# Splitting two weight loads of the last expert but one, and moving a register read behind expert 8's loads

## The chip, the cores and the metric

The kernel runs on one core of one Trainium2 chip. The metric is the device time of one execution in microseconds (us). TensorE (PE) multiplies, VectorE (DVE), ScalarE (ACT) and GpSimd (POOL) do the elementwise work, SyncE (SP) issues nearly all loads from device memory. Before the change three executions took 1123.03, 1123.43 and 1123.51 us; the median is 1123.43 us. A difference of 0.2% (about 2.2 us) is what such a measurement can tell from no change.

## The reference

One layer over 256 tokens of width 1024: a modulated RMS norm, one input projection shared by a convolution branch and a bidirectional linear recurrence, an output projection with a gated residual; then a second modulated norm and a mixture of 32 experts, of which every token takes two out of one group of eight; at the end a gated residual and a final RMS norm. All is float32. The part that the change touches is the mixture:

```python
def swiglu_expert(xb, w1, w3, w2):
    return (jax.nn.silu(xb @ w1) * (xb @ w3)) @ w2

def hier_moe(h, wg, bg, we, be, w1, w3, w2):
    ...                         # group, two experts and gates of each token
    yb = lax.map(run, (xb, blk_e)).reshape(n_rows, D)      # run: swiglu_expert of each block
    return jnp.zeros_like(h).at[tok_buf].add(yb * gate_buf[:, None])
```

Each expert has three matrices of 1024 x 1024 float32, 4 MB each; all 96 are read once, 403 MB.

## The kernel before

**Front part.** The first 198 us hold norms, projections, convolution, recurrence and routing. Every expert then gets 64 token slots (`CAP`). Should an expert have more tokens than that, a loop at the program's end (`rest`) does the remainder; whether it runs is decided by `nmax`, the largest token count, which `nc.values_load` reads into a register of every engine (line 1038). With these inputs the loop doesn't run.

**Experts.** The loop over e = 0 to 30 does for each expert `up(w1)`, SiLU, `up(w3)`, a product, four transposes, and `up(w2)`. `up` reads its matrix in two tiles of 128 partitions x 4096 float32, that is 16 KB in each partition and 2048 KB in all (line 874), and issues eight matmuls for each tile (line 877). So there are 6 such loads for an expert and 186 in the loop. For odd e the gather of the next four experts' tokens stands between `up(w3)` and `up(w2)` (line 789), for even e the scatter of the two experts before (lines 899, 904).

**The ring of tiles.** The tiles are nine buffers, `wide0` to `wide8`, taken in a fixed order (`WORDER`). A load may start once PE has done with the tile that used the buffer nine loads earlier. SP issues all loads in program order, and it stops at the first instruction whose wait isn't over. The loads' completion semaphores are eight, used in rotation (`DMAHW0` to `DMAHW7` below): a load also waits until the load eight before it has landed.

**The token count.** After expert 1, DVE reduces the slot positions to one number (lines 1031 to 1036), with one transpose on PE in between, and writes it to `fmi`. Behind the loads of expert 2, every engine's own queue holds the register read of `fmi` (line 1038); behind it SP issues a small load of the final gain `fgbc` (line 1040), which two matmuls of expert 2's end use (line 1043).

**The last expert.** Expert 31 is loaded in smaller pieces: eight of 1024 KB (line 1059, matmuls in line 1062), four of 512 KB with 4 KB in a partition (line 1106), and four of 512 KB by columns (line 1115; matmuls of both in line 1100). After the last pieces come the scatter (line 1131), the norm and the store of the output.

Of the kernel before, what the change touches and what calls it, by code (L numbers as in the profile page):

```python
# [17 lines left out]
E = 32  # L18
# [51 lines left out]
def hybrid_layer(ctx: ExitStack, tc: tile.TileContext, sp_d, x_d, c_d, bada_d, rb_d, fg_d, gw_d,  # L70
# [3 lines left out]
    dma = nc.sync.dma_start  # L74
# [10 lines left out]
    def bank():  # L85
        return psp.tile([128, 512], F32, name="bank")

    def slot():
        return wp.tile([128, 2048], F32, name="slot")
# [82 lines left out]
    xs = [slot().rearrange("p (k t) -> p k t", k=8) for _ in range(2)]  # L172
# [76 lines left out]
    def load_wz(q):  # L249
        w, hi, lo = slot(), slot_r(), slot_r()  # L250
        dma(w.rearrange("p (k n) -> p k n", k=2),
            win_d[q * 256:(q + 1) * 256, 0:1024].rearrange("(k p) n -> p k n", p=128))
        wz.append([v.rearrange("p (k n) -> p k n", k=2) for v in (hi, lo)])
        return w, hi, lo
# [25 lines left out]
    def slot_r():  # L280
        return r(slot())
# [59 lines left out]
    w = load_wz(0)  # L341
# [3 lines left out]
    for q in range(4):  # L345
        ks = range(2 * q, 2 * q + 2)
        if q < 3:
            w = load_wz(q + 1)
# [9 lines left out]
    for i in range(2):  # L358
        w, hi, lo = slot(), slot_r(), slot_r()
# [173 lines left out]
    def rowbc(dst, rows, j0):  # L533
        for j in range(2):
            pr = bank()
            r = 32 * (j0 + j)
            P.matmul(pr, ones[r:r + 1, :], rows[r:r + 1, :], start=True, stop=True, tile_position=(r, 0))
            S.copy(dst[:, j * 512:(j + 1) * 512], pr)
# [230 lines left out]
    def onehot(oh, t, g):  # L769
        V.tensor_tensor(oh[:, t], iota1[:, None, :].to_broadcast([128, 4, CAP]),  # L770
                        posm[:, t, g * 4:g * 4 + 4, None].to_broadcast([128, 4, CAP]), OP.is_equal)
# [12 lines left out]
    def quad(k):  # L784

        return slice(k // 4 * 512 + k % 4, k // 4 * 512 + 512, 4)

    def gather_mm(pg, i, k, oh, t):
        P.matmul(pg[:, i * 256:(i + 1) * 256], xn[:, t, quad(k)],  # L789
                 oh[:, t].rearrange("p e s -> p (e s)"), start=t + i == 0, stop=t == 1 and i == 1,  # L790
                 skip_group_check=True)

    def gather_out(xg, pg, i, k):
        if i == 0:
            S.activation(xg[:, k], pg[:, i * 256:(i + 1) * 256], AF.Identity, scale=gsp[:, 0, k:k + 1],  # L795
                         bias=gsp[:, 1, k:k + 1])
        else:
            V.tensor_scalar(xg[:, k], pg[:, i * 256:(i + 1) * 256], gsp[:, 0, k:k + 1], gsp[:, 1, k:k + 1],  # L798
                            OP.mult, OP.add)

    def gather_new(dt=F32):
        return (ohp.tile([128, 2, 4, CAP], dt, name="oh"),
                xgt().rearrange("p (k s) -> p k s", k=8))
# [18 lines left out]
    def route(t):  # L822
# [5 lines left out]
                 w=load_wl, z=gelu_mm, e=gelu_act, m=lru_out, M=ln_mean,  # L828
# [5 lines left out]
    for word in ORDER.split():  # L834
        word, _, n = word.partition("*")
# [13 lines left out]
    def wide():  # L849
        n = WORDER[turn[0] % WIDE]  # L850
        turn[0] += 1
        return wx.tile([128, 4096], F32, name=f"wide{n}")
# [14 lines left out]

        return piece

    def up(w_d, e, xs):  # L870
        ps = bank()
        for k4 in range(2):
            w = wide().rearrange("p (k n) -> p k n", k=4)
            dma(w, w_d[e, k4 * 512:(k4 + 1) * 512, :].rearrange("(p k) n -> p k n", p=128))
            for i in range(4):
                for h in range(2):
                    P.matmul(ps[64 * h:64 * h + 64, :], xs(k4 * 4 + i), w[:, i, h * 512:(h + 1) * 512],  # L877
                             start=k4 + i == 0, stop=k4 * 4 + i == 7, tile_position=(0, 64 * h))
        return ps

    def sel_build(e0):
        so = mo.tile([128, 2, 2, CAP], F32, name="so")
        for t in range(2):
            for i in range(2):
                V.tensor_scalar(so[:, t, i], iota1, posm[:, t, e0 + i:e0 + i + 1],
                                gate[:, t, e0 + i:e0 + i + 1], OP.is_equal, OP.mult)
        return so

    def sel_turn(so):
        pt = bank()  # L890
        for t in range(2):
            P.transpose(pt[:, t * 128:(t + 1) * 128], so[:, t].rearrange("p e s -> p (e s)"), ident)
        st = mo.tile([128, 256], F32, name="st")
        S.copy(st, pt[:, 0:256])
        return st

    def scatter_mm(st, yy, t, h):
        pz = bank()
        P.matmul(pz, st[:, t * 128:(t + 1) * 128], yy[:, h * 512:(h + 1) * 512], start=True, stop=True)  # L899
        return pz  # L900

    def scatter_add(pz, t, h):
        q = slice(h * 512, (h + 1) * 512)
        V.tensor_tensor(x1[:, t, q], x1[:, t, q], pz, OP.add)  # L904
# [64 lines left out]
    for e in range(E - 1):  # L969
        xs = lambda k: xg[:, k, (e % 4) * CAP:(e % 4 + 1) * CAP]  # L970
        if e % 2 == 0:
            so = sel_build(e)
        gat = e % 2 == 1 and e // 4 < E // 4 - 1
        if gat and e % 4 == 1:
            noh, nxg = gather_new()
            onehot(noh, 0, e // 4 + 1)
            onehot(noh, 1, e // 4 + 1)
        pa = up(w1_d, e, xs)
        sl = mo.tile([128, 512], F32, name="sl", bufs=1)
        S.activation(sl, pa, AF.Silu)  # L980
        if e == 0:
            rowbc(g2bc, g2r, 2)
        if e % 2 == 0:
            st = sel_turn(so)
        pb = up(w3_d, e, xs)
        gg = sl
        V.tensor_tensor(gg, sl, pb, OP.mult)  # L987
        pzs = []
        k0 = (e % 4) // 2 * 4
        if gat:  # L990
            pgs = [bank(), bank()]
            for k in range(3):
                for t in range(2):
                    gather_mm(pgs[k // 2], k % 2, k0 + k, noh, t)
            for k in range(2):
                gather_out(nxg, pgs[0], k, k0 + k)
        elif e % 2 == 0 and e:
            for n in range(3):
                pzs.append(scatter_mm(*prev, *TH[n]))
                if n < 2:  # L1000
                    scatter_add(pzs[n], *TH[n])
        pt = bank()
        for j in range(4):
            P.transpose(pt[:, j * 128:(j + 1) * 128], gg[:, quad(j)], ident)  # L1004
        gt = mo.tile([128, 4, 128], F32, name="gt", bufs=1)
        V.tensor_copy(gt[:, 0:2], pt[:, 0:256])  # L1006
        S.copy(gt[:, 2:4], pt[:, 256:512])  # L1007
        if gat:
            for t in range(2):
                gather_mm(pgs[1], 1, k0 + 3, noh, t)  # L1010
            for k in range(2, 4):
                gather_out(nxg, pgs[1], k % 2, k0 + k)
        elif pzs:
            pzs.append(scatter_mm(*prev, *TH[3]))
            for n in range(2, 4):
                scatter_add(pzs[n], *TH[n])
        gts = lambda f: gt[:, f % 4, 64 * (f // 4):64 * (f // 4) + 64]
        py = up(w2_d, e, gts)
        if e % 2 == 0:
            yy = mo.tile([128, D], F32, name="yy", bufs=1)  # L1020
        for h in range(2):
            o = (e % 2) * 64
            V.tensor_tensor(yy[o:o + 64, h * 512:(h + 1) * 512], py[64 * h:64 * h + 64, :],  # L1023
                            g2bc[64 * h:64 * h + 64, h * 512:(h + 1) * 512], OP.mult)
        if e % 2 == 1:
            prev = (st, yy)
        if e % 4 == 3:
            xg = nxg
        if e == 1:
            fmx = mo.tile([128, 1], F32, name="fmx")  # L1030
            V.tensor_reduce(fmx, posm.rearrange("p t e -> p (t e)"), AX.X, OP.max)
            fpt = bank()
            P.transpose(fpt[0:1, 0:128], fmx, ident)
            fmr = mo.tile([1, 1], F32, name="fmr")
            V.tensor_reduce(fmr, fpt[0:1, 0:128], AX.X, OP.max)
            V.tensor_copy(fmi, fmr)
        if e == 2:
            nmax = nc.values_load(fmi[0:1, 0:1], min_val=0, max_val=T)
        if e == 2:
            dma(fgbc[0:1, :], fg_d)  # L1040
            for j in range(2):
                pr = bank()
                P.matmul(pr, ones[0:1, :], fgbc[0:1, j * 512:(j + 1) * 512], start=True, stop=True)
                S.copy(fgbc[:, j * 512:(j + 1) * 512], pr)
# [8 lines left out]
    e = E - 1  # L1053
# [49 lines left out]
    for f2 in range(2):  # L1103
        w = piece(2048).rearrange("p (k n) -> p k n", k=2)
# [120 lines left out]
```

## Time and profile before

| what | value |
|---|---|
| time, median of 3 runs | 1123.43 us |
| the profiled execution's own time | 1124.29 us |
| its span, first to last instruction | 1122.5 us |
| PE busy | 1001.9 us, 89% |
| DVE, ACT, POOL busy | 308.7, 173.7, 104.1 us |
| moved by DMA | 445.21 MB, 397 GB/s over the span |
| mean granted PE clock | 0.984 of full speed |

The span is cut into stretches by the views below. "DMA share" is the mean busy share of the core's 16 DMA engines in a stretch; it can come out a little over 1 because a packet is counted where it starts. The chain of waits is followed back from the last instruction, at each step to what released it. A wait that the profile puts down to an instruction ended when that instruction's semaphore was updated.

### The profile page before, as it was taken

The numbers are of one execution on the slowest core, as the hardware profiler recorded it, in microseconds if no ns is written. First come the engines' busy times: TensorE is split into PE (matmuls) and PEld (weight loads), VectorE is DVE, ScalarE is ACT, GpSimd is POOL, SyncE is SP. The second block draws the span as 40 slices with busy tenths as digits, with TensorE's granted clock in tenths as the row PEclk, the third lists the DMA queues.
The fourth block names the chain that finished last, engine by engine and source line by source line (L and its number), as shares of the span: only waits on it lengthen the run. The fifth ranks groups of instructions, "written<-read, shape, count | busy, mean of one in ns | idle before, by whom it ended". The sixth has DMA issues, their size and how long they took to land.

```text
span 1122.5 us, 11836 instructions
## 1 busy us (share of the span) xinstructions
PE 1001.9 (89%) x4947; PEld 447.2 (40%) x4947; DVE 308.7 (27%) x625; ACT 173.7 (15%) x329; POOL 104.1 (9%) x107
## 2 busy tenths in 40 slices
PE   7889999999999999888888998988898989898795
PEld 6764547343434333323333333333333333232244
DVE  4788975221121112111211121112121111111113
ACT  3457944100000000000000000000000000000002
POOL 2487443000000000000000000000000000000001
PEclk9899997999999999999999999999999999999999
DMA  9756759989999999999999999999999999999994
GB/s 362 266 227 267 295 214 409 391 371 411 431 430 431 430 431 430 430 431 431 429 431 430 431 432 430 430 431 430 430 431 430 430 431 430 431 431 430 431 410 184
DMA packets 50015, 445.21 MB, mean 397 GB/s; under 512 B 4083, under 2 KB 14371, under 8 KB 24100
## 3 DMA queue, kind: packets, MB, share of 16 engines
q1 hardware_dynamic: 49746, 443.84, 94.2%
q8 instruction: 41, 0.67, 0.2%
q10 hardware_dynamic: 210, 0.55, 0.1%
q14 instruction: 18, 0.15, 0.0%
HBM read 443.32 MB, written 1.05 MB: 396 GB/s over the span
## 4 chain that ended last, share of the span: by engine, by line
DMA 57%; PE 33%; DVE 5%; POOL 1%; issue 1%; ACT 1%; SPq 1%; DVEq 0%; POOLq 0%; ACTq 0%
DMA wide<-in_w_dram 57%; PE bank L877 18%; PE bank L789 3%; PE bank L680 2%; PE bank L899 2%; PE bank L377 2%; PE bank L331 1%; PE bank L511 1%; DVE bank L469 1%; PE bank L815 1%; PE bank L315 1%; DVE slot L293 1%; PE bank L1004 1%; POOL slot L303 1%; SPq L1059 1%
## 5 line engine op out<-in xcount | busy, mean ns | idle before, releaser
L877 PE MATMUL bank<-wide,xg 128*64 128x512 f32 x1984 | 448.4, 596 | 78.6 <-DMA wide<-in_w_dram 78.5
L877 PEld LDWEIGHTS bank<-wide,xg 128*64 128x64 f32 x1984 | 141.4, 137 | 370.1 <-issue 256.7
L877 PE MATMUL bank<-wide,gt 128*64 128x512 f32 x992 | 219.9, 595 | 2.9 <-DMA wide<-in_w_dram 2.3
L987 DVE TENSOR_TENSOR sl<-sl,bank 128x512 f32<-128x512 f32 x31 | 21.3, 687 | 467.4 <-issue 443.8
L877 PEld LDWEIGHTS bank<-wide,gt 128*64 128x64 f32 x992 | 68.6, 137 | 141.8 <-issue 137.4
L1023 DVE TENSOR_TENSOR yy<-bank,g2bc 64x512 f32<-64x512 f32 x62 | 42.7, 688 | 193.4 <-PE bank L877 193.0
L1142 POOL TENSOR_TENSOR xg<-x,fgbc 128x256 f32<-128x256 f32 x6 | 4.2, 728 | 914.1 <-DMA wide<-in_w_dram 912.8
L980 ACT ACTIVATE sl<-bank 128x512 f32<-128x512 f32 x31 | 18.5, 597 | 437.5 <-PE bank L877 437.5
L789 PE MATMUL bank<-oh,xn 128*128 128x256 f32 x224 | 61.1, 416 | 0.0
L789 PEld LDWEIGHTS bank<-oh,xn 128*128 128x128 f32 x224 | 54.4, 327 | 11.4 <-issue 11.4
L899 PE MATMUL bank<-yy,st 128*128 128x512 f32 x120 | 58.0, 606 | 0.0
L1007 ACT COPY gt<-bank 128x256 f32<-128x256 f32 x31 | 11.6, 373 | 219.4 <-DVE gt L1006 219.4
L904 DVE TENSOR_TENSOR x<-x,bank 128x512 f32<-128x512 f32 x60 | 39.7, 683 | 7.1 <-PE bank L899 7.1
L795 ACT ACTIVATE xg<-bank,gsp 128x256 f32<-128x256 f32 x32 | 17.9, 564 | 153.7 <-PE bank L789 149.2
L303 POOL TENSOR_TENSOR slot<-slot 128x2048 fp32r<-128x2048 f32 x7 | 32.3, 4627 | 34.1 <-ACT slot L298 24.9
L331 PE MATMUL bank<-slot 128*128 128x256 f32 x192 | 28.7, 309 | 7.6 <-ACT slot L292 6.4
L899 PEld LDWEIGHTS bank<-yy,st 128*128 128x128 f32 x120 | 20.6, 191 | 26.5 <-issue 23.2
L331 PEld LDWEIGHTS bank<-slot 128*128 128x128 f32 x192 | 26.5, 211 | 9.7 <-ACT slot L292 7.4
L798 DVE TENSOR_SCALAR xg<-bank,gsp 128x256 f32<-128x256 f32 x32 | 17.2, 543 | 47.3 <-ACT xg L795 47.2
L377 PE MATMUL bank<-slot 128*128 128x512 f32 x96 | 22.9, 394 | 1.5 <-POOL slot L303 1.5
L1004 PEld LDWEIGHTS bank<-ident,sl 128*128 128x128 f32 x124 | 19.5, 204 | 11.1 <-issue 7.1
L487 POOL TENSOR_TENSOR xn<-xn,fgbc 128x256 f32<-128x256 f32 x30 | 22.5, 750 | 2.3
(249 smaller groups left out, 690.1 us busy)
## 6 DMA issues: line engine op xcount, KB each, us to landing
wide<-in_w_dram SPq DMA_DIRECT2D x186, 2048.0 KB, 38.7
slot<-in_wada_dram SPq DMA_DIRECT2D x16, 1024.0 KB, 6.2
slot<-in_wada_dram SPq DMA_DIRECT2D x16, 512.0 KB, 8.8
slot<-in_win_dram SPq DMA_DIRECT2D x8, 1024.0 KB, 9.1
wide<-in_w_dram SPq DMA_DIRECT2D x8, 1024.0 KB, 22.6
slot<-in_wout_dram SPq DMA_DIRECT2D x4, 1024.0 KB, 8.7
wide<-in_w_dram SPq DMA_DIRECT2D x8, 512.0 KB, 11.8
x<-in_x_dram SPq DMA_DIRECT2D x2, 512.0 KB, 4.4
```

The source lines that it names most:

```text
L303: en.tensor_tensor(lo, w, f(hi), OP.subtract)
L331: P.matmul(pvg[ct][:, i * T:(i + 1) * T], wz[k // 2][wi][:, k % 2, c:c + 128], x[k // 4][:, k % 4, 0:T], start=k + i + n == 0, stop=k == 7 ...
L377: P.matmul(pu, w, x[k // 4][:, k % 4], start=k + n == 0, stop=k == 7 and n == 2)
L487: G.tensor_tensor(acc, acc, p, OP.add)
L680: P.matmul(p, m[:, q], w[:, c:c + 512], start=first and n == 0, stop=len(done) == 8 and n == len(passes) - 1)
L789: P.matmul(pg[:, i * 256:(i + 1) * 256], xn[:, t, quad(k)], oh[:, t].rearrange("p e s -> p (e s)"), start=t + i == 0, stop=t == 1 and i == ...
L877: P.matmul(ps[64 * h:64 * h + 64, :], xs(k4 * 4 + i), w[:, i, h * 512:(h + 1) * 512], start=k4 + i == 0, stop=k4 * 4 + i == 7, tile_positi ...
L899: P.matmul(pz, st[:, t * 128:(t + 1) * 128], yy[:, h * 512:(h + 1) * 512], start=True, stop=True)
L904: V.tensor_tensor(x1[:, t, q], x1[:, t, q], pz, OP.add)
L987: V.tensor_tensor(gg, sl, pb, OP.mult)
L1004: P.transpose(pt[:, j * 128:(j + 1) * 128], gg[:, quad(j)], ident)
L1023: V.tensor_tensor(yy[o:o + 64, h * 512:(h + 1) * 512], py[64 * h:64 * h + 64, :], g2bc[64 * h:64 * h + 64, h * 512:(h + 1) * 512], OP.mult)
```

## The change

Two edits. `up` gets the numbers of partitions that its two tiles' main loads cover. For expert 30's `w2` they are 96 and 112 in place of 128 and 128; the remaining 32 and 16 partitions come by loads of 8 partitions each, four and two. The bytes are the same. And the register read of the token count is issued for e = 8 in place of e = 2.

```diff
-    def up(w_d, e, xs):
+    def up(w_d, e, xs, parts=(128, 128)):
+
         ps = bank()
         for k4 in range(2):
             w = wide().rearrange("p (k n) -> p k n", k=4)
-            dma(w, w_d[e, k4 * 512:(k4 + 1) * 512, :].rearrange("(p k) n -> p k n", p=128))
+            src = w_d[e, k4 * 512:(k4 + 1) * 512, :].rearrange("(p k) n -> p k n", p=128)
+            dma(w[0:parts[k4]], src[0:parts[k4]])
+            for o in range(parts[k4], 128, 8):
+                dma(w[o:o + 8], src[o:o + 8])
...
-        py = up(w2_d, e, gts)
+        py = up(w2_d, e, gts, (96, 112) if e == E - 2 else (128, 128))
...
-        if e == 2:
+        if e == 8:
             nmax = nc.values_load(fmi[0:1, 0:1], min_val=0, max_val=T)
```

SP's queue behind expert 2's last loads, before (`wide3`, `wide8`: expert 2's `w2`; `fmi`: the token count; `wide0`, `wide7`: expert 3's `w1`):

```order
L874 DMA wide3_2011<-in_w2_dram 128x4096
L874 DMA wide8_2021<-in_w2_dram 128x4096
L1038 TENSOR_LOAD fmi_1740
L1038 ISA x2
L1040 DMA fgbc_111<-in_fg_dram 1x1024
L874 DMA wide0_2056<-in_w1_dram 128x4096
L874 DMA wide7_2066<-in_w1_dram 128x4096
```

The same place on SP in the changed kernel:

```order
L876 DMA wide3_2011<-in_w2_dram 128x4096
L876 DMA wide8_2021<-in_w2_dram 128x4096
L1044 DMA fgbc_111<-in_fg_dram 1x1024
L876 DMA wide0_2042<-in_w1_dram 128x4096
L876 DMA wide7_2052<-in_w1_dram 128x4096
```

The register read is gone from here; the load of `fgbc` and expert 3's loads follow expert 2's directly. SP's queue behind expert 8's last loads in the changed kernel (`wide3`, `wide8`: expert 8's `w2`; `wide0`, `wide7`: expert 9's `w1`):

```order
L876 DMA wide3_2589<-in_w2_dram 128x4096
L876 DMA wide8_2599<-in_w2_dram 128x4096
L1042 TENSOR_LOAD fmi_1740
L1042 ISA x2
L876 DMA wide0_2631<-in_w1_dram 128x4096
L876 DMA wide7_2641<-in_w1_dram 128x4096
```

The read now stands here, and in the other engines' queues at the same place of the program. SP's queue at expert 30's `w2` and the first loads of expert 31, with the semaphores that each load waits for, before (the first two rows are expert 30's `w2`):

```order
L874 DMA wide_4688<-in_w_dram 128x4096 [waits DMAHW5_49,PE_49]
L874 DMA wide_4698<-in_w_dram 128x4096 [waits DMAHW6_49,PE_49]
L1059 DMA wide_4717<-in_w_dram 128x4x512 [waits DMAHW7_49,PE_49]
L1059 DMA wide_4717<-in_w_dram 128x4x512 [waits DMAHW0_49]
L1059 DMA wide_4738<-in_w_dram 128x4x512 [waits DMAHW1_49,PE_49]
```

And in the changed kernel (the first eight rows are expert 30's `w2`):

```order
L876 DMA wide_4688<-in_w_dram 96x4096 [waits DMAHW5_49,PE_49]
L878 DMA wide_4688<-in_w_dram 8x4096 [waits DMAHW6_49]
L878 DMA wide_4688<-in_w_dram 8x4096 [waits DMAHW7_49]
L878 DMA wide_4688<-in_w_dram 8x4096 [waits DMAHW0_49]
L878 DMA wide_4688<-in_w_dram 8x4096 [waits DMAHW1_49]
L876 DMA wide_4702<-in_w_dram 112x4096 [waits DMAHW2_49,PE_49]
L878 DMA wide_4702<-in_w_dram 8x4096 [waits DMAHW3_49]
L878 DMA wide_4702<-in_w_dram 8x4096 [waits DMAHW4_49]
L1063 DMA wide_4723<-in_w_dram 128x4x512 [waits DMAHW5_49,PE_49]
L1063 DMA wide_4723<-in_w_dram 128x4x512 [waits DMAHW6_49]
```

Two loads have become eight, and all eight semaphores have gone round once: expert 31's first load waits for the semaphore of the 96-partition load, where before it waited for that of a load of expert 29.

## Rows read from the trace of the kernel before

**Rows 1.** The page, part 2: DMA share in tenths and GB/s, 40 equal slices.
```profile
DMA  9756759989999999999999999999999999999994
GB/s 362 266 227 267 295 214 409 391 371 411 431 430 431 430 431 430 430 431 431 429 431 430 431 432 430 430 431 430 430 431 430 430 431 430 431 431 430 431 410 184
```
**Rows 2.** The page, part 4: the chain of waits, shares of the span by engine.
```profile
DMA 57%; PE 33%; DVE 5%; POOL 1%; issue 1%; ACT 1%; SPq 1%; DVEq 0%; POOLq 0%; ACTq 0%
```
**Rows 3.** The chain in order of time: start us, us, what.
```profile
372.36 3.61 PE bank L877 x16
375.99 35.48 DMA wide<-in_w_dram
...
1067.54 3.68 PE bank L877 x16
...
1092.59 12.83 DMA wide<-in_w_dram
...
1105.46 1.09 PE bank L1100 x16
```
**Rows 4.** SP's timeline, 226 to 256 us: start us, us, line, operation, tile, count.
```profile
226.39 7.20 SPq L874 DMA_DIRECT2D wide<-in_w_dram  x3
251.77 0.31 SPq L1040 DMA_DIRECT2D fgbc<-in_fg_dram  x1
252.18 2.14 SPq L874 DMA_DIRECT2D wide<-in_w_dram  x4
```
**Rows 5.** SP's waits, 225 to 256 us: us in total, times, longest us.
```profile
SPq L1038 <- DVE so L885: 17.7, 1, 17.7
```
**Rows 6.** Windows: length, busy of PE PEld DVE ACT POOL, PEclk, DMA share, GB/s.
```profile
246.00:248.00 2.00, 2.00 (x12) 0.53 (x8) 0.00 (x0) 0.00 (x0) 0.00 (x0) 1.00 1.01 434
248.00:250.00 2.00, 0.27 (x2) 0.00 (x0) 1.60 (x3) 0.00 (x0) 0.00 (x0) 1.00 0.33 139
250.00:252.00 2.00, 1.91 (x9) 0.71 (x11) 1.31 (x6) 0.00 (x0) 0.00 (x0) 1.00 0.02 8
252.00:254.00 2.00, 2.00 (x12) 0.72 (x10) 0.00 (x0) 0.00 (x0) 0.00 (x0) 1.00 0.49 109
254.00:256.00 2.00, 2.00 (x12) 0.65 (x10) 0.00 (x0) 0.00 (x0) 0.00 (x0) 1.00 0.97 385
```
**Rows 7.** PE's timeline, 231 to 256 us.
```profile
236.58 3.18 PE L789 MATMUL bank<-oh,xn 128*128 128x256 f32 x12
...
241.18 7.09 PE L877 MATMUL bank<-wide,gt 128*64 128x512 f32 x32
```
**Rows 8.** Line 1038: duration ns min/median/max, first and last start us.
```profile
L1038 SPq TENSOR_LOAD <-fmi x1: 466/466/466, 250.9 to 250.9; - x1
...
L1038 PEldq TENSOR_LOAD <-fmi x1: 490/490/490, 271.4 to 271.4; - x1
L1038 DVEq TENSOR_LOAD <-fmi x1: 545/545/545, 275.9 to 275.9; - x1
```
**Rows 9.** DMA issues: queue, operation, count, KB each, median us to landing.
```profile
wide<-in_w_dram SPq DMA_DIRECT2D x186, 2048.0 KB, 38.7
...
bada<-in_bada_dram ACTq DMA_DIRECT2D x1, 24.0 KB, 3.4
```
**Rows 10.** Windows of the steady state and of the last loads, columns as in rows 6.
```profile
600.00:610.00 10.00, 10.00 (x42) 3.69 (x38) 3.68 (x6) 0.37 (x1) 0.00 (x0) 1.00 1.01 431
...
1104.00:1106.00 2.00, 1.63 (x26) 1.42 (x28) 0.58 (x2) 0.00 (x0) 0.00 (x0) 1.00 0.59 208
1106.00:1108.00 2.00, 2.00 (x24) 1.45 (x20) 1.35 (x4) 0.32 (x1) 0.22 (x1) 1.00 0.23 73
```
**Rows 11.** The page, part 3: packets, MB, share of 16 engines' span.
```profile
q8 instruction: 41, 0.67, 0.2%
```
**Rows 12.** SP's waits over the whole span.
```profile
SPq L874 <- DMA wide<-in_w_dram: 566.1, 141, 5.8
```
**Rows 13.** Line 874 on SP: duration ns min/median/max, first and last start.
```profile
L874 SPq DMA_DIRECT2D wide<-in_w_dram x186: 327/328/425, 155.4 to 1036.9; - x186
```

## The prediction

> **What bounds the kernel now.** I read the page's slices first, then the chain of waits, then SP's timeline and waits where the slices dip, and last the windows around the dip and around the end. From slice 11 to slice 38 the slices show one flat rate, 429 to 432 GB/s with all 16 DMA engines busy [rows 1]; 57% of the chain is the weight loads [rows 2], and from 376 us on the chain is load after load [rows 3], to the last pieces at 1105 us. Before 376 us PE sets the chain, because nine tiles were loaded ahead while PE was still on the front part, and it works off that stock. So after about 200 us the end of the program hangs on one thing: when the stream of loads has moved its last byte. An idle stretch of that stream is paid for in full, wherever it lies, since PE catches up with the stream at 372 us and then only waits for it. After the last pieces there is a tail of PE, ACT and DVE work from 1105.46 us to the end at 1122.5 us, which neither edit touches.
>
> The stream has one hole in that part. SP issues three loads up to 233.6 us and the next at 251.8 us [rows 4]; between them it waits 17.7 us for the token count [rows 5]. What had been issued runs out: the share is 1.01 up to 248 us, then 0.33, 0.02 and 0.49 in steps of 2 us, and 0.97 again from 254 us [rows 6].
>
> **Moving the register read.** It removes SP's 17.7 us stop. What is late next is the buffer: the load behind the read reuses the tile that PE gives back when expert 1's `w3` is done, at about 236.6 us, where the gather begins [rows 7]; the next two reuse the tiles of expert 1's `w2`, given back at 244.7 and 248.3 us (half and all of 241.18 + 7.09). A 2048 KB load takes 2.097 MB / 431 GB/s = 4.87 us. The stream has work until about 248.7 us as it is (a third of the window from 248 to 250); the load at 236.6 carries it to 253.5, the one at 244.7 to 258.4, the one at 248.3 to 263.3. Each is issued about 9 us or more before the stream needs it, so the hole closes.
>
> Its size, by engine time: (1.01 - 0.33) + (1.01 - 0.02) + (1.01 - 0.49) + (1.01 - 0.97) = 2.23, times 2 us = 4.5 us. By bytes: (431 - 139) + (431 - 8) + (431 - 109) + (431 - 385) = 1083, times 2 / 431 = 5.0 us. The engine that finished last gains less than the mean, because in the kernel before all engines start again together behind the hole: only about 3 us pass with next to none busy (all of 250 to 252 us, and half of 252 to 254). Bounds 3 and 5.0 us; I take 4.6, near the mean, since engines that were late at 249 us need not be those that are last at 1105 us.
>
> At its new place the read holds SP for 0.47 us and about 0.4 us behind it [rows 4, 8]; the loads in flight there cover 38.7 us [rows 9]. Queued behind it on PE are expert 9's matmuls: 0.49 us on the weight loads' queue [rows 8], in a stretch where PE waits for the stream anyway; DVE's 0.55 us falls into idle time. `fmi` has been written long before, so nobody waits for it. Cost 0; should the cover fail, 0.9 us. The load of `fgbc` goes out about 18 us earlier and is wanted behind expert 2, so it gives nothing and costs nothing.
>
> **Splitting expert 30's `w2`.** Bytes and issue order stay; six issues are added, 6 x 0.33 = 2 us of SP [rows 13], hidden by the same 38 us of loads in flight. What changes is how the rows (16 KB, one partition) fall on the 16 engines. A full load gives each engine 8 rows in 4.87 us, 0.61 us a row. The loads of 96 and 112 give 6 and 7. A load of 8 rows can use eight engines at most; if it is always the same eight, these get 6 + 4 + 7 + 2 = 19 rows in place of 16 and the other eight 13: 3 rows or 1.8 us more, and 1.8 us less.
>
> That is worth something only if the engines don't finish together, and they don't: in the last stretch the share is 0.59 and then 0.23 over 4 us [rows 10], where about half of the engines still carry packets and the others are through. A cause stands on the page: 41 instruction reads take 0.2% of 16 engines' span, 36 us of engine time [rows 11]. If eight engines carry them, each is 4.5 us later than the rest. No view names the engines. Perfect levelling of that stretch would gain (1 - 0.59) x 2 + (1 - 0.23) x 2 = 2.4 us; the split moves 3 rows, so it gains 1.8 us if the eight with the small loads are those that are early, and loses 1.8 us if they are those that are late. I take the gain, as a judgement with odds of about four to one and not as a reading, and keep both ends.
>
> [...]
>
> **The added wait.** SP holds eight completion semaphores in rotation and already waits for them 141 times [rows 12]. Now expert 31's first load waits for the 96-partition load. The load before that one lands at 1067.5 us (PE starts on it at 1067.54 [rows 3]), so the 96 rows land at 1067.5 + 6 x 0.61 = 1071.2 us, and expert 31's data can start some 1 to 1.5 us later, as behind the hole (issue at 252.18 us, packets from about 253 [rows 4, 6]), at about 1072.5. By then even an engine that is 4 us ahead still holds 4 + 7 + 2 rows (7.9 us from 1067.2: till 1075). If the early engines are those without small loads they hold 7 rows (till 1071.5) and idle for a microsecond, but they are not last. Cost 0, at worst 1 us.
>
> Sum: -4.6 - 1.8 = -6.4 us. The profiled execution took 1124.29 us, 1122.5 us of it span; it becomes 1117.9. The median of the runs lies 0.86 us lower, 1123.43, so the forecast is 1117.0 us.
>
> **Rivals.** (a) The split does nothing: the small loads spread, or the late engines are not a fixed half. For it: no view shows which engines are late. Time 1123.43 - 4.6 = 1118.8 us. (b) The split loads the late half: 1123.43 - 4.6 + 1.8 = 1120.6 us. (c) The hole closes but is given back, because PE still has its stock and buffers come free late: against it speak the 9 us of lead above. Then only the split counts: 1121.6 us, or 1123.4 without it.
>
> (d) Slower: a load of 8 rows is slow in itself. It writes 8 neighbouring partitions; if these can take in no more than two engines' worth at a time, a row lasts four times as long, 2.4 us. The engines with the small loads then need 13 + 6 x 4 = 37 row times in place of 16, 21 x 0.61 = 12.8 us more; 4 us of lead absorb a part, and the stream ends 8.8 us later: 1123.43 - 4.6 + 8.8 = 1127.6 us. The change turns slower from where one small load lasts 2.8 row times (1.7 us): (13 + 6 x 2.8 - 16) x 0.61 - 4 = 4.4, about the hole's gain. For it: the only narrow load with a landing time, 24 KB on 48 partitions, took 3.4 us [rows 9]. Against it: that is issue to landing of a load by itself, and loads that follow each other overlap such times. [...]
>
> **How the numbers follow.** Forecast 0.52, (a) 0.17, (b) 0.10, (c) 0.05, (d) 0.16; (d) in full has 0.08, and as much in part, between 1119 and 1126. A change of 0.2%, 2.2 us, is what can be told from none: faster means below 1121.2, slower above 1125.7. Faster: 0.52 + 0.17 + 0.10 and 0.03 of (d), 0.82. Within: (c) and 0.05 of (d), 0.10. Slower: 0.08. The likeliest case's own range is 1116.0 to 1118.6: the hole's bounds of 3 and 5.0 us around 4.6 give +1.6 and -0.4, and the split's best of 2.4 us a further -0.6. For eight in ten I go from 1115.5 up through (a) and (b) to 1121.8.
>
> **What would show it.** Right: no register read on SP near 251 us, a share near 1.01 in all windows from 240 to 260 us, every later landing about 4.6 us earlier, and at the end a share that falls from 1 to 0 within 2 us in place of 4. Wrong: the hole is still there or comes back behind expert 3; or the share after expert 30's small loads falls to half for several us while PE waits for them, which would be (d); or a longer half-share stretch at the end, which would be (b).

## The result, and the profile after

The changed kernel takes 1136.93 us (median of 4 runs, 1133.25 to 1139.72) against 1123.47 us before (median of 4): ratio 1.0115, interval 1.0092 to 1.0137. It is slower by 13.5 us, where 6.4 us less was forecast. The profiled execution has a span of 1135.9 us and an own time of 1137.73 us. One of the two edits did what was expected and the other cost 20 us.

The page's slices of the changed kernel (28.4 us each), which answer to [rows 1]:

```profile
DMA  9767759999999999999999999999999999999994
GB/s 361 262 229 304 279 233 374 430 431 429 430 433 429 430 431 431 430 430 432 430 431 431 430 430 429 432 432 430 428 432 431 429 431 433 430 429 433 226 321 171
```

The dip of before at slices 9 and 10 (371, 411) is gone: 431, 429. A new one stands near the end: 226 and 321. The DMA share shows nothing of it, it is 9 throughout. The engines are busy all that time and move half as much. By bytes the two slices lose (430 - 226 + 430 - 321) / 430 x 28.4 = 20.7 us; the same stretch of before lost 1.4 us, (431 - 410) / 431 x 28.1.

Windows where the hole was, columns as in [rows 6]:

```profile
246.00:248.00 2.00, 0.46 (x4) 0.00 (x0) 1.47 (x3) 0.00 (x0) 0.00 (x0) 1.00 0.94 403
248.00:250.00 2.00, 1.72 (x9) 0.71 (x11) 1.45 (x7) 0.00 (x0) 0.00 (x0) 1.00 1.09 467
250.00:252.00 2.00, 2.00 (x12) 0.61 (x10) 0.00 (x0) 0.00 (x0) 0.00 (x0) 1.00 1.03 442
252.00:254.00 2.00, 2.00 (x12) 0.68 (x10) 0.00 (x0) 0.00 (x0) 0.00 (x0) 1.00 0.94 401
254.00:256.00 2.00, 2.00 (x12) 0.62 (x10) 0.00 (x0) 0.39 (x1) 0.00 (x0) 1.00 0.99 426
```

Where the share had been 0.33, 0.02 and 0.49 it is 1.09, 1.03 and 0.94. The register read at its new line, which answers to [rows 8]:

```profile
L1042 SPq TENSOR_LOAD <-fmi x1: 499/499/499, 388.3 to 388.3; - x1
...
L1042 PEldq TENSOR_LOAD <-fmi x1: 490/490/490, 424.7 to 424.7; - x1
L1042 DVEq TENSOR_LOAD <-fmi x1: 546/546/546, 429.3 to 429.3; - x1
```

SP reads 36 to 41 us ahead of PE and DVE and doesn't wait there; the slices around it stay at 430.

Windows over expert 30's `w2` and the first pieces of expert 31, same columns:

```profile
1050.00:1055.00 5.00, 4.02 (x18) 1.27 (x18) 0.00 (x0) 0.54 (x2) 0.00 (x0) 1.00 1.09 426
1055.00:1060.00 5.00, 3.52 (x16) 1.06 (x16) 0.00 (x0) 0.32 (x2) 0.00 (x0) 1.00 0.97 206
1060.00:1065.00 5.00, 0.13 (x2) 0.00 (x0) 0.00 (x0) 0.00 (x0) 0.00 (x0) 1.00 1.08 174
1065.00:1070.00 5.00, 2.53 (x6) 0.77 (x8) 0.00 (x0) 0.00 (x0) 0.00 (x0) 0.50 0.96 203
...
1080.00:1085.00 5.00, 3.42 (x10) 1.35 (x12) 0.00 (x0) 0.00 (x0) 0.00 (x0) 0.71 1.03 237
1085.00:1090.00 5.00, 1.93 (x8) 0.41 (x4) 0.00 (x0) 0.00 (x0) 0.00 (x0) 0.95 1.03 315
```

From such a row the time of one 16 KB packet can be worked out: 16 engines x 16.384 KB = 262 KB, times share / rate. Up to 1055 us it is 262 x 1.09 / 426 = 0.67, about the 0.61 of the steady state [rows 10]; in the next rows 1.23, 1.63 and 1.24 us. So the packets became two to three times as long; no engine was waiting for work.

PE follows the stream; where it waits for a load, it starts when that load has landed. Its timeline there (the last column is the wait before, and for whom):

```profile
1056.48 3.65 PE L881 MATMUL bank<-wide,xg 128*64 128x512 f32 x16 [1.70 <-DMA wide<-in_w_dram]
1067.47 5.81 PE L881 MATMUL bank<-wide,xg 128*64 128x512 f32 x16 [7.34 <-DMA wide<-in_w_dram]
...
1091.66 5.35 PE L881 MATMUL bank<-wide,gt 128*64 128x512 f32 x16 [4.73 <-DMA wide<-in_w_dram]
```

The first two rows are the tiles of expert 30's `w3`, both whole loads; the last is the second tile of its `w2`. From the first to the last three tiles land in 35.2 us, where three whole loads take 14.6 (3 x 4.87): 20.6 us more. The tile that was issued just ahead of the split loads, itself whole, lands 11.0 us after the one before it, in e1 4.9 us after it (1054.59 and 1059.45 in e1's timeline). Behind the pair nothing more is lost: from the first of these rows to the last landing of the stream the changed kernel needs 63.2 us and e1 42.8, again 20.4 us more.

After the wait of 7.34 us the granted clock is 0.50 in the window from 1065 to 1070, and one tile's matmuls (sixteen records) take 5.81 us in place of 3.65. That costs nothing by itself, since the chain's last links are again loads, and the last one ends at 1106.64 + 13.01 = 1119.65 us, 14.2 us later than before [rows 3]:

```profile
1093.20 13.42 DMA wide<-in_w_dram
1106.64 13.01 DMA wide<-in_w_dram
```

One more reading is needed to add things up. Executions differ in the front part: the first matmul of expert 0 starts at 198.2 us before, at 196.4 after and at 195.5 in the first experiment (the number ahead of "to"; one row of each kernel's matmul line):

```profile
L877 PE MATMUL bank<-wide,xg x1984: 592/592/644, 198.2 to 1070.6; 128*64 128x512 f32 x199
```
```profile
L881 PE MATMUL bank<-wide,xg x1984: 592/592/1113, 196.4 to 1072.7; 128*64 128x512 f32 x199
```
```profile
L877 PE MATMUL bank<-wide,xg x1984: 592/592/1117, 195.5 to 1062.5; 128*64 128x512 f32 x199
```

The span less this start, called the rest below, leaves the front's scatter out. Each rest comes from one profiled execution, so differences of about half a microsecond between rests are not to be read. All kernels that compute the layer:

| kernel | median us | ratio, interval | span - start = rest | rest against e1 |
|---|---|---|---|---|
| before | 1123.43 | 1 | 1122.5 - 198.2 = 924.3 | +5.1 |
| after | 1136.93 | 1.0115 (1.0092 to 1.0137) | 1135.9 - 196.4 = 939.5 | +20.3 |
| e1_read_only | 1117.03 | 0.9942 (0.9926 to 0.9959) | 1114.7 - 195.5 = 919.2 | 0 |
| e2_split_only | 1143.42 | 1.0176 (1.0159 to 1.0193) | 1141.9 - 197.5 = 944.4 | +25.2 |
| e3_rest_whole | 1134.24 | 1.0095 (1.0078 to 1.0112) | 1131.3 - 196.4 = 934.9 | +15.7 |
| e5_quarters | 1117.45 | 0.9947 (0.9931 to 0.9962) | 1118.1 - 199.5 = 918.6 | -0.6 |
| e6_level | 1122.84 | 0.9996 (0.9977 to 1.0014) | 1123.0 - 198.1 = 924.9 | +5.7 |
| e7_halves | 1136.19 | 1.0111 (1.0077 to 1.0145) | 1134.6 - 201.2 = 933.4 | +14.2 |
| e8_early | 1135.55 | 1.0103 (1.0072 to 1.0134) | 1136.1 - 198.0 = 938.1 | +18.9 |
| e9_level_two | 1124.60 | 1.0003 (0.9986 to 1.0021) | 1124.7 - 199.4 = 925.3 | +6.1 |
| e10_level_four | 1131.16 | 1.0064 (1.0043 to 1.0086) | 1129.6 - 198.3 = 931.3 | +12.1 |

Each ratio is against the runs of before on the same chip, whose median was 1122.77 to 1124.19 us.

### The profile page after: what moved, and what is told of

Its sections match the earlier page's. It is cut to its first block, busy times and chain, and to the rows that moved or that the text cites. A ratio compares the mean times of both kernels' runs of the same rounds, so it can differ in the third digit from the quotient of the medians.

```text
span 1135.9 us, 11845 instructions
## 1 busy us (share of the span) xinstructions
PE 1008.9 (89%) x4947; PEld 449.7 (40%) x4947; DVE 308.7 (27%) x625; ACT 173.7 (15%) x329; POOL 104.1 (9%) x107
## 4 chain that ended last, share of the span: by engine, by line
DMA 53%; PE 37%; DVE 5%; SPq 1%; POOL 1%; issue 1%; ACT 1%; DVEq 0%; POOLq 0%; ACTq 0%
DMA wide<-in_w_dram 53%; PE bank L881 21%; PE bank L789 3%; PE bank L680 2%; PE bank L903 2%; PE bank L377 2%; SPq L1063 1%; PE bank L331 1%; PE bank L511 1%; DVE bank L469 1%; PE bank L815 1%; PE bank L1008 1%; PE bank L315 1%; DVE slot L293 1%; POOL slot L303 1%
## 5 line engine op out<-in xcount | busy, mean ns | idle before, releaser
L881 PE MATMUL bank<-wide,gt 128*64 128x512 f32 x992 | 223.5, 603 | 10.2 <-DMA wide<-in_w_dram 5.0
L331 PE MATMUL bank<-slot 128*128 128x256 f32 x192 | 28.4, 308 | 6.2 <-ACT slot L292 4.9
L903 PEld LDWEIGHTS bank<-yy,st 128*128 128x128 f32 x120 | 20.6, 191 | 26.7 <-issue 23.4
```

The source lines that it names most:

```text
L331: P.matmul(pvg[ct][:, i * T:(i + 1) * T], wz[k // 2][wi][:, k % 2, c:c + 128], x[k // 4][:, k % 4, 0:T], start=k + i + n == 0, stop=k == 7 ...
```

## The experiments

**e1 and e2: one edit each.** e1 moves the register read alone, e2 splits expert 30's `w2` alone.

```diff
-        if e == 2:
+        if e == 8:
             nmax = nc.values_load(fmi[0:1, 0:1], min_val=0, max_val=T)
```

> Only the register read is moved; expert 30's w2 is loaded as before. Both theories of the slowdown put it into the split loads, so both expect the hole of 4.5 to 5.0 us to close and about 4.6 us less than before: 1118.8 us, between 1118 and 1121. A rival, that the moved read itself costs (queued behind expert 8, or the stream's engines no longer start together), expects 1123 us or more.

> Only expert 30's w2 is split; the register read stays behind expert 2. If the two edits simply add, this is the changed kernel's 1136.9 us plus the hole's 4.6 us: 1141 us, 1138 to 1145. If the moved read had a part in the slowdown, it is below 1136 us.

The read alone gives 1117.03 us, 6.8 less than before and a little better than the range expected; the split alone 1143.42, 19.6 more and within its range. The sum, +12.8, is close to the 13.5 measured for both: the edits don't act on each other. In the rests of the table the read is worth 5.1 us and the split 20.1 (e2 against before) or 20.3 (after against e1). By this reckoning some 1.7 of the read's 6.8 us are the front's scatter, whose start lies between 195.5 and 201.2 us over these profiles, later than before in e5 though the read is moved there too. In e1 the window of the hole is full:

```profile
246.00:256.00 10.00, 8.64 (x41) 2.97 (x43) 2.50 (x9) 0.86 (x2) 0.00 (x0) 1.00 1.00 428
```

**e3: the small loads joined.** The remaining 32 and 16 partitions come as one load each.

```diff
-            for o in range(parts[k4], 128, 8):
-                dma(w[o:o + 8], src[o:o + 8])
+            if parts[k4] < 128:
+                dma(w[parts[k4]:128], src[parts[k4]:128])
```

> As the changed kernel, but the remaining 32 and 16 partitions come by one load each in place of loads of 8. Theory N (only the loads of 8 partitions are slow, the main loads run at the full 0.61 us a row): the loss goes almost wholly, 1118 to 1121 us, and the windows over expert 30's w2 show 400 GB/s or more. Theory M (any load of fewer than 128 partitions runs slowly, the 96-partition load too): the tile of 96 and 32 takes about twice 4.9 us, the second tile somewhat longer too, so 1123 to 1130 us, and a rate near 200 GB/s already while the 96-partition load is at work.

1134.24 us, above the ranges of both theories; 15.7 of the 20.3 us remain without a load of 8 partitions. So the loads of 8 are not the main cause: pieces of 96, 112, 32 and 16 neighbours lose most of it.

```profile
1055.00:1060.00 5.00, 3.50 (x16) 1.06 (x16) 0.00 (x0) 0.37 (x2) 0.00 (x0) 1.00 1.04 220
...
1080.00:1085.00 5.00, 1.36 (x8) 0.22 (x4) 0.00 (x0) 0.00 (x0) 0.00 (x0) 1.00 1.00 222
```

**e4: loads by themselves.** No computation; the output is zeros. Stages of equal loads, each waited for before the next begins; one execution.

```python
dma(ws[n][0:96], src(4 + n)[0:96])           # likewise 0:128, 0:112, 0:64, 96:128, 96:104
dma(ws[n][0:128:2], src(18 + n)[0:64])       # every second; likewise 0:128:4, 96:128:4, 0:128:16
```

> Loads alone, no expert is computed and the output is zeros: thirteen stages, each a row of equal loads of 16 KB rows that lands before the next stage begins; the first and the last are four full loads of 128 partitions, expected at about 420 GB/s. Theory N (only narrow loads are slow): 96, 112 and 64 partitions at 400 GB/s or more, 32 near that, only the 8-partition loads slow, 50 to 110 GB/s for neighbouring partitions. [...] A third theory, that the place of the rows in device memory decides: 96 partitions from rows 32 KB apart run at another rate than from rows 16 KB apart, and partitions every second or fourth run like neighbouring ones.

One window within each stage (length, DVE, POOL, PEclk, DMA share, GB/s):

```profile
305.00:310.00 5.00, 0.00 (x0) 0.00 (x0) 1.00 0.99 426
45.00:60.00 15.00, 0.00 (x0) 0.00 (x0) 1.00 1.01 237
75.00:90.00 15.00, 0.00 (x0) 0.00 (x0) 1.00 1.00 256
105.00:120.00 15.00, 0.00 (x0) 0.00 (x0) 1.00 1.02 208
137.00:147.00 10.00, 0.00 (x0) 0.00 (x0) 1.00 1.01 433
157.00:169.00 12.00, 0.00 (x0) 0.00 (x0) 1.00 0.98 199
181.00:187.00 6.00, 0.00 (x0) 0.00 (x0) 1.00 1.01 423
194.00:206.00 12.00, 0.00 (x0) 0.00 (x0) 1.00 0.51 55
215.00:220.00 5.00, 0.00 (x0) 0.00 (x0) 1.00 0.45 144
225.00:233.00 8.00, 0.00 (x0) 0.00 (x0) 1.00 0.50 104
240.00:260.00 20.00, 0.00 (x0) 0.00 (x0) 1.00 0.92 167
```

| partitions of one load | GB/s | one packet, us (262 x share / rate) |
|---|---|---|
| 0 to 127 | 426 | 0.61 |
| 0 to 95 | 237 | 1.12 |
| 0 to 111 | 256 | 1.02 |
| 0 to 63 | 208 | 1.28 |
| 64, every second one | 433 | 0.61 |
| 96 to 127 | 199 | 1.29 |
| 32, every fourth one | 423 | 0.63 |
| 96 to 103 | 55 | 2.43 |
| 8, every fourth one (96, 100, ...), issued 0.69 us apart | 144 | 0.82 |
| 8, every sixteenth one | 104 | 1.26 |
| the changed pair | 167 | 1.44 |

The same number of partitions goes at full rate or at half, by which ones they are: 64 neighbours 208 GB/s, every second one 433; 32 neighbours 199, every fourth one 423. So neither the number of rows nor the size of the load decides alone, and theory N falls. 0 to 63 is hardly faster than the 32 neighbours 96 to 127 (208 against 199), and 8 neighbours take four times as long a packet as a full load (2.43 us against 0.61); why, no view shows. Another stage had the source rows of a 96-partition load 32 KB apart: 234 GB/s against 237, so this spacing in device memory changes next to nothing, and the third theory falls too.

**e5: four loads of a tile, every fourth partition.**

```diff
+                for r in range(4):
+                    dma(w[r:128:4], src[r:128:4])
```

e4's loads of 32 partitions, every fourth one, ran at 423 GB/s and its whole loads at 426; at these rates the time is that of e1, 1117.0 us.

> As the changed kernel (register read moved), but both tiles of expert 30's w2 come as four loads of 32 partitions each, every fourth one (0, 4, 8, ... then 1, 5, 9, ...). [...] Rival N (a load of fewer than 128 partitions is slow whichever they are, or more and smaller loads are): half rate for the two tiles at least, 9.7 us more, 1126.7 us. Rival S (rows 64 KB apart in device memory are slow): the same 1126.7 us.

1117.45 us, 0.4 above e1; the rest is 0.6 us below that of e1: no loss from cutting a load in four, and none from rows 64 KB apart in device memory. Rivals N and S, at 1126.7 us, fall.

```profile
1060.00:1065.00 5.00, 3.78 (x20) 1.14 (x18) 0.00 (x0) 0.00 (x0) 0.00 (x0) 1.00 1.01 429
```

**e7: two loads of a tile, 64 neighbours each.**

```diff
+                for o in (0, 64):
+                    dma(w[o:o + 64], src[o:o + 64])
```

> As e5_quarters, but each of the two tiles comes as two loads of 64 neighbouring partitions (0 to 63, then 64 to 127); every engine gets 4 rows of each. [...] Rival N' (what hurts is that 96 and 112 rows don't fall on the engines by eights, or that small loads use eight engines): 1117.0 us.

1136.19 us, 14.2 us in the rests: most of what the change loses, with 64 rows in each load (four for each of the 16 engines, if they are dealt evenly) and no small load at all. Rival N' falls.

```profile
1060.00:1065.00 5.00, 3.65 (x16) 1.06 (x16) 0.00 (x0) 0.12 (x1) 0.00 (x0) 1.00 1.01 229
...
1085.00:1090.00 5.00, 0.36 (x2) 0.00 (x0) 0.00 (x0) 0.00 (x0) 0.00 (x0) 1.00 0.99 219
1090.00:1095.00 5.00, 4.51 (x14) 1.43 (x16) 0.00 (x0) 0.00 (x0) 0.00 (x0) 0.66 1.05 400
```

It is more than e4's rate for 64 neighbours gives, 4 x 1.049 MB / 208 GB/s = 20.2 us in place of 9.7, 10.5 us more: the half rate lasts 30 us (6.5 MB), but the halves hold only 4.2 MB. PE's timeline shows whose the rest is (first and second tile of expert 30's `w3`, second tile of its `w2`):

```profile
1061.21 3.65 PE L883 MATMUL bank<-wide,xg 128*64 128x512 f32 x16 [1.63 <-DMA wide<-in_w_dram]
1071.70 5.96 PE L883 MATMUL bank<-wide,xg 128*64 128x512 f32 x16 [6.84 <-DMA wide<-in_w_dram]
...
1090.48 5.11 PE L883 MATMUL bank<-wide,gt 128*64 128x512 f32 x16 [5.13 <-DMA wide<-in_w_dram]
```

The three tiles take 29.3 us, 14.7 more than three whole loads, so the whole loss lies here. The whole load issued just ahead of the halves lands 10.5 us after the one before it, in place of 4.9: 2.097 MB in 10.5 us are 200 GB/s, close to the 206 to 229 of the windows from 1060 to 1090 us. Why a whole load takes this rate is not shown; no view names the engines.

**e8: the split in the middle.** The change with `e == 15` in place of `e == E - 2`.

> As the changed kernel, but the split (96 and 112 partitions, then loads of 8) stands at expert 15's w2, in the middle of the stream, and expert 30's w2 is whole. The stream is the bound from 372 us on, so a loss there is paid in full: 1136.6 us, as in the changed kernel, or 1132.3 us if it is what the pair cost in the run of loads alone (25 us in place of 9.7). Rival P (the loss is large because it meets the end, where nothing can be made up): less than half of it remains, below 1127 us.

1135.55 us, near the 1136.6 expected and far from rival P; 18.9 us in the rests. The loss is not one of the end. The slices of its page:

```profile
GB/s 361 261 223 286 279 234 385 418 429 432 431 428 431 433 428 431 432 431 429 431 431 381 223 429 433 430 428 433 429 431 429 433 429 430 431 431 430 429 388 182
```

381 and 223 lose (430 - 381 + 430 - 223) / 430 x 28.4 = 16.9 us, and the 18.9 in the rests show that nothing is made up in the stream that follows.

**e6, e9 and e10: the levelling without neighbours.** Tiles cut into three loads of 32 and four of 8 partitions, every fourth one; in e6 both tiles of expert 30's `w2`, in e9 the first tile of the `w2` of experts 20 and 28, in e10 of experts 8, 14, 20 and 26.

```diff
+                for r in range(3):
+                    dma(w[r:128:4], src[r:128:4])
+                for o in range(3, 128, 32):
+                    dma(w[o:min(o + 32, 128):4], src[o:min(o + 32, 128):4])
```

> As e5_quarters, but the last of the four loads of each tile is cut into four loads of 8 partitions, every fourth one (3 to 31, 35 to 63, 67 to 95, 99 to 127). Eight engines then get 6 + 4 + 6 + 4 = 20 rows and the others 12, 4 rows or 2.4 us away from 16. [...] Rival N (small loads are slow whichever partitions they take): 8 x 2.4 us on eight engines in place of 8 x 0.61, some 14 us more, 1131 us.

> As e6_level, but the cut tiles (three loads of 32 and four of 8 partitions, every fourth one) are not the two of expert 30's w2 one behind the other: they are the first tile of expert 20's w2 and the first of expert 28's, 144 MB and more of whole tiles apart and away from the end. The eight small loads and the rows that they move between the engines are those of e6_level. Theory W (e6_level lost its 5.7 us because fourteen loads in a row take all eight completion semaphores, so that too few bytes are in flight and engines run dry): with only seven in a row the loss goes to 0 to 1 us, and the levelling shows: 1117 - 2.4 = 1114.6 us if the eight engines of the small loads are the early ones, 1119.4 us if they are the late ones. Rival X (a load of 8 partitions costs what it costs in e6_level, 5.7 / 8 = 0.7 us each, wherever it stands): 1122.8 us as e6_level.

> As e9_level_two, with four cut tiles, the first of the w2 of experts 8, 14, 20 and 26: sixteen small loads, 8 rows or 4.9 us from 8 engines to the other 8. Theory W: the levelling overshoots; if the late half was 4 us behind it is now about 1 us ahead of the other, 1116 us (1115 to 1118); if the small loads fall on the late half, 1117 + 4.9 = 1121.9 us. Rival X: 16 x 0.7 = 11.4 us more than the read alone, 1128.4 us.

e6's 1122.84 us is far from rival N's 1131, and it is more than the levelling by itself could do: four rows of 0.61 us, 2.4 us either way around e1's 1117.0. e9 and e10 ask why. (Between e9's cut tiles lie 48 loads, 101 MB, not 144.) The rests are 5.7, 6.1 and 12.1 us above that of e1, for 8, 8 and 16 small loads: 0.71, 0.76 and 0.76 us for each, wherever they stand. Every cut tile holds four of them, so it may as well be some 3 us for a cut tile. Theory W (too few semaphores) fell, rival X came out. In e6 the share does drop, which had suggested W:

```profile
1060.00:1065.00 5.00, 3.37 (x18) 0.93 (x16) 0.00 (x0) 0.00 (x0) 0.00 (x0) 1.00 0.86 256
...
1070.00:1075.00 5.00, 3.94 (x17) 1.26 (x16) 1.08 (x2) 0.35 (x1) 0.00 (x0) 1.00 0.73 224
```

In e9, with a single cut tile, the share is 1.00 over the four rows together and the packets are longer, 262 x 0.96 / 229 = 1.10 us in the second row:

```profile
770.00:772.00 2.00, 1.75 (x8) 0.63 (x10) 0.00 (x0) 0.00 (x0) 0.00 (x0) 1.00 1.17 311
772.00:774.00 2.00, 2.00 (x11) 0.60 (x8) 0.00 (x0) 0.00 (x0) 0.00 (x0) 1.00 0.96 229
774.00:776.00 2.00, 2.00 (x5) 0.90 (x6) 1.51 (x3) 0.00 (x0) 0.00 (x0) 1.00 1.05 287
776.00:778.00 2.00, 2.00 (x8) 0.86 (x6) 1.36 (x3) 0.30 (x1) 0.00 (x0) 1.00 0.83 246
```

**e11: small loads among whole ones.** By themselves loads of 8 partitions, every fourth one, took 0.82 us a packet (e4), and in e9 the packets took 1.10 us in a window with a share of 0.96; so the guess was that it depends on what they meet.

```python
dma(ws[n], src(base + n)[0:128])
for r in range(2):
    dma(ws[4 + n][first + r:first + 32:4], src(base + n)[128 + 8 * r:136 + 8 * r])   # first = 0, 64, 32, 96
```

> Loads alone, no computation; the output is zeros. Stages: six full loads; then four times a full load with two loads of 8 partitions, every fourth one, behind it: partitions 0 to 31, then the same with 64 to 95, with 32 to 63 and with 96 to 127; then four times a full load with one of partitions 0 to 95, and with one of 0 to 63; six full loads. A 16 KB packet's time follows from a window as 262 x share / GB/s (16 engines x 16.384 KB). [...] Rival F (any load of 8 partitions among full ones slows the packets, some 0.75 us of stream each as in e9_level_two): all four stages alike, 0.8 us and more. [...]

Windows, in the order: whole loads alone; with small ones to 0 to 31; to 64 to 95; to 32 to 63; to 96 to 127; whole loads alternating with 0 to 95.

```profile
267.00:291.00 24.00, 0.00 (x0) 0.00 (x0) 1.00 1.01 433
45.00:60.00 15.00, 0.00 (x0) 0.00 (x0) 1.00 1.01 433
72.00:93.00 21.00, 0.00 (x0) 0.00 (x0) 1.00 1.01 353
105.00:120.00 15.00, 0.00 (x0) 0.00 (x0) 1.00 0.99 425
135.00:156.00 21.00, 0.00 (x0) 0.00 (x0) 1.00 1.01 345
168.00:212.00 44.00, 0.00 (x0) 0.00 (x0) 1.00 1.01 309
```

Packets of 0.61 us for 0 to 31 and 32 to 63, of 0.75 and 0.77 for 64 to 95 and 96 to 127: the four stages are not alike, and rival F falls. Why the two halves of the partitions differ is not shown, since no view names the engines. The price can be estimated: a whole load and two small ones are 2.36 MB, 5.4 us at 433 GB/s and 6.7 at 353, so a small load to the upper half costs 0.6 us, and one to the lower half next to nothing. Two of the four small loads of a cut tile in e9 write the upper half; that is 1.2 of the 3 us that the tile lost. The last row has 0.86 us in the mean, and its rate goes up and down: 437 GB/s in the window from 180 to 183 us, 273, 251 and 262 in the next three of 3 us; whole loads alone have 433, and loads of 0 to 95 alone 237 (e4).

## Why the prediction was wrong

**What bounds the kernel** was right: what the stream loses is lost at the end, 20.3 us at expert 30 and 18.9 at expert 15 (e8).

**Moving the register read** was right in mechanism and nearly in size: 4.6 us had been taken between 3 and 5.0; measured are 5.1 in the rests of e1 and before, and 5.3 to 6.8 in the medians of e5 and e1. The estimate by bytes, 5.0, was the nearer one, but the rests scatter by as much as the two estimates differ. The read costs nothing at its new place, as said.

**Splitting expert 30's `w2`** is the step that failed. It stood in the sum with -1.8 us and measured +20.3. The sentence that went wrong: "A full load gives each engine 8 rows in 4.87 us, 0.61 us a row. The loads of 96 and 112 give 6 and 7." The time of a row was wrong: 1.12 us in a load of 96 and 1.02 in one of 112 (e4), not 0.61. How many rows each engine got, no view shows. A time read from whole loads was carried over to loads that write other sets of partitions. From e4 the pair's parts are 6.6 us for the 96 (1.573 MB / 237 GB/s), 7.2 for the 112 (1.835 MB / 256) and 6 x 2.4 for the small ones, 28.2 us one after the other; issued together they ran at 167 GB/s, 25.1 us for 4.19 MB in place of 9.7, which is 15.4 us more. In the kernel it was 20.3 us more. No run shows the 1.8 us of the sum: that a small load reaches no more than eight engines fits e4 (its eight loads of 96 to 103 were issued from 190.1 to 192.5 us, and from 194 to 206 the share was 0.51), but that these are the early ones at the end was a judgement, and what the runs showed for the split is the loss. The prediction also took the load ahead of the split as untouched ("lands at 1067.5 us", before the hole's gain); in the changed kernel that tile took 11.0 us in place of 4.9.

**The levelling** isn't to be had in this way either. With partitions every fourth one, where e4's loads of 32 run at 423 GB/s and its loads of 8 at 0.82 us a packet, a small load still cost 0.7 to 0.8 us (e6, e9, e10), where the levelling was to gain. In e11 the packets take 0.75 and 0.77 us in the mean beside small loads to 64 to 127, and 0.61 beside those to 0 to 63; by its price this is less than half of the cost, and the rest of it is open. The premise that a fixed half of the engines is late was not tested. The sign named for the end, a share that falls to nothing within 2 us, didn't come: it is 0.88, 0.20 and 0.11 in steps of 2 us from 1116 us in the changed kernel.

**The added wait** cost little that can be seen: in the twelve windows of 5 us from 1050 to 1110 us of the changed kernel the share is 1.00 in the mean, against 1.01 in the steady state, so the engines had work.

**Rival (d)** had the right kind of cause and was given 0.16. It was too small, since it put four row times on the small loads alone, 8.8 us, and left 96 and 112 at full rate. Its four row times were right (2.43 us against 4 x 0.61). The order of evidence was at fault: the trace had no narrow large load, and the value was taken from the rows of whole loads, the nearest there were. The two engines' worth that it put on eight neighbouring partitions was an assumption, for which the trace of before has no number; e4 shows 55 GB/s, close to two sixteenths of a whole load's 426 (53). For 96 and 112 neighbours e4 shows 237 and 256 GB/s.

Left open: why 96 and 112 neighbours run at little more than half rate (237 and 256 GB/s of 426); why e11's packets are longer beside small loads to 64 to 127 (0.75 and 0.77 us) and not beside those to 0 to 63 (0.61); why the three tiles take 4 to 5 us more than their loads take by themselves (35.2 against 4.9 + 25.1 in the changed kernel, 29.3 against 4.9 + 20.2 in e7), while in e11 a whole load and one of 0 to 95 took 11.9 us together (3.67 MB / 309 GB/s) against 4.8 + 6.6 by themselves; and which of the engines were late at the end of the kernel before.

**The version to keep** is e1: 1117.03 us, 0.9942 of before (0.9926 to 0.9959), 20 us less than the changed kernel.

## What to carry to other kernels

A load's rate depended here on which partitions it writes, not on its bytes alone (64 neighbours 208 GB/s, every second one 433; e4). Where a load of 128 partitions has to be cut, four loads of every fourth partition were free here (e5, 0.6 us below e1 in the rests); blocks of neighbours ran at 0.6 of the full rate or less (e4, 55 to 256 GB/s of 426), and the whole load ahead of them was slowed too (10.5 us in e7 and 11.0 in the changed kernel, in place of 4.9). A busy share of 1 says that the DMA engines are occupied, not how much they move (e4: 1.01 at 237 and at 433 GB/s); read it beside GB/s. In this stream, which sets the end, the idle stretch was worth its bytes over the rate (5.0 us, and 5.1 in the rests), so look for the one queue that stops issuing.

## What the hardware showed that was not expected

- 96 and 112 neighbouring partitions run at 237 and 256 GB/s, little more than 64 (208).
- Among whole loads with small ones the packets take 0.75 and 0.77 us in the mean when the small ones write partitions 64 to 127, and 0.61 when they write 0 to 63 (e11).
- The slow stretch takes in the whole load issued ahead of the split ones: that tile landed 10.5 us after the one before it in e7 and 11.0 in the changed kernel, in place of 4.9.
